# A decoder block on one core: the compressed branch's inner products in four pieces of sixteen records, without the break in the middle of each

## The chip, the cores and the metric

The kernel runs on one core of one Trainium2 chip. The metric is the device time of one execution in microseconds (us); the median of three runs is compared. Engines are called as in the profile: PE (TensorE matmul), PEld (its weight load), DVE (VectorE), ACT (ScalarE), POOL (GpSimd), SP (SyncE, which issues the loads here).

## What is computed

One block of a decoder, with 256 tokens of 1024 channels in f32. Two token mixers read one normed and modulated input h through one projection; their outputs are merged by gates and go through one output projection; a gated MLP follows. Cut to what matters:

```
mod = silu(c) @ ada_w + ada_b                      # six vectors of 1024
h   = rmsnorm(x) * (1 + scale_m) + shift_m
p   = split(h @ w_in)      # nsa_q, k/v for three branches, gates, mla parts, merge_a, merge_b
kc  = compress(p.k_cmp);  vc = compress(p.v_cmp)   # blocks of 32 tokens, stride 16: 15 per group
      # compress: gelu((block + pos) @ w1) @ w2,  w1 is 2048 x 256
o_nsa = g0 * softmax_c(q kc) vc + g1 * softmax_selected + g2 * softmax_window   # 16 heads
o_mla = mla(rmsnorm(cq) @ w_uq, rmsnorm(ckv) @ w_ukv, k_rope)                   # 8 heads
y   = sigmoid(merge_a) * o_nsa + sigmoid(merge_b) * o_mla
x   = x + gate_m * (y @ w_o)
x   = x + gate_f * convglu(rmsnorm(x) * (1 + scale_f) + shift_f)                # D_FF = 2816
out = rmsnorm(x)
```

With 256 tokens there are four selection blocks and all are taken, so the selected branch is causal attention; the window of 512 holds all tokens as well.

## The kernel before

Activations stand transposed, channels on partitions and the 256 tokens along the free axis. Most weights are loaded raw (tiles of 128x1024, 512 KB, five buffers `raw`) in one order on SP's queue, and split into a high part on ACT (`hi`, line 136) and a low part on DVE (`lo`, line 137); a product is then three on PE (`mm3`, lines 179 to 182, on top of `mm`, lines 176 and 177). The tiles of the compressed branch's `w1` are used raw.

The program's stages are: the first norm and the part of the adaLN vectors that it needs; the combined input projection; the loop over eight pairs of NSA heads; eight MLA heads, with the merge_b projections between; w_o with the residual; the feed-forward part from about 238 us on, in 22 tiles; the last norm.

The pair loop carries a second stream of work. `ORDER` (line 54) is the order of steps of one pair: turns T, logits L, values V, the finish C, and five F. At each F, `fill(1)` does the next step of `WORK` (line 53): "C0 A A A A A A A L0 C1 L1 A C2 A L2 C3 N M0 KR CK CS M1 A CR M2 Q0 CL UK A A Q1 M3 M7 M5 M6 UV M4". A step that is a generator takes a slot for each of its yields and one for its end. There are 8 x 5 = 40 slots; what is left over is done by `fill(99)` behind the loop. C0 to C3 are `cmp_mlp(c)` (from line 658): the inner layer of the compressed branch, 32 products in all, which add up in one PSUM bank `ms` (64 rows for the keys, 64 for the values, 256 columns). C3 goes on with the gelu and two transposes (line 683). L0 to L2 and M0 to M7 are projections (the MLA latents, merge_a), N the two MLA norms (lines 222, 259, 260, 271 and 273), KR the rotary key, CK the compressed keys, CS the logits and softmax of the compressed branch (lines 726 to 742), CR the turning of its rows (lines 749 and 751), Q0, Q1, UK and UV MLA's inner projections. A is one product of an adaLN tile with the condition, on DVE (a gemv, line 378), whose tile is loaded at line 534 into one of two buffers `ad`; A takes no slot.

CR sets `done`. A head pair that finishes before that is added to the list `late`: its compressed part is made by CL afterwards, two products to a pair and an add on DVE (line 768). A pair that finishes later has these two products in its own bank `o`.

What an engine does in which order is settled by a scheduler: each instruction has a priority of its kind (`PR` and `PK`, lines 50 and 51; the inner products are of the kind CM), and of what is ready the most urgent one goes first. So the slot of a step sets about where it can stand, not its exact place. In the MLA heads, line 956 is the merge (tanh gate times `o`), line 957 the add to the NSA output, lines 958 and 959 its split; line 992 is the first residual of w_o.

Of the kernel before, what the change touches and what calls it, by code (L numbers as in the profile page):

```python
# [56 lines left out]
def body(tc, a, out, dbg=None):  # L57
    nc = tc.nc
    with ExitStack() as ctx:
# [12 lines left out]
        def prio(key):  # L72
            o = PR[PK.index(key)]
            return tc.high_priority(offset=o) if o else nullcontext()
# [23 lines left out]
        def t1(tag, dt=F32, shape=(128, 256), bufs=2):  # L98
            return tp.tile(list(shape), dt, tag=tag, name=nm(tag), bufs=bufs)

        def bank(tag):
            return pa.tile([128, 512], F32, tag=tag, name=nm(tag), bufs={"lg": 2, "pt": 2, "mm": 2}.get(tag, 1))

        def free(ap, dims, off=0):
            return bass.AP(tensor=ap.tensor, offset=ap.offset + off, ap=[ap.ap[0]] + [list(d) for d in dims])
# [36 lines left out]
        def nextw():  # L142
            prefetch(depth[0])
            return pending.pop(0)
# [31 lines left out]
        def mm(o, l, r, start, stop, **kw):  # L176
            nc.tensor.matmul(o, l, r, start=start, stop=stop, **kw)  # L177
# [480 lines left out]
        def cmp_mlp(c):  # L658

            if c == 0:  # L660
                hps.append(bank("ms"))
            ps = hps[0]
            w1 = [nextw() for _ in range(2)]
            for m4 in range(4):
                m = c * 4 + m4
                for kv in range(2):
                    with prio("CM"):
                        mm(ps[kv * 64:kv * 64 + 64, 0:256], free(TB[kv][:, m // 8, :], [[8, 64]], m % 8),
                           w1[kv][:, m4 * 256:m4 * 256 + 256], m == 0, m == 15, skip_group_check=True)
                if m4 == 1:  # L670
                    yield
            if c < 3:
                return
            hx, u = t1("zh", bufs=3), t1("zh", bufs=3)
            nc.scalar.activation(hx[:], ps[:, 0:256], AF.Copy, scale=0.5)
            nc.vector.tensor_tensor(u[:], hx[:], hx[:], ALU.mult)
            nc.vector.tensor_scalar(u[:], u[:], 4 * 0.044715, 1.0, ALU.mult, ALU.add)
            nc.vector.tensor_tensor(u[:], u[:], hx[:], ALU.mult)
            nc.scalar.activation(u[:], u[:], AF.Tanh, scale=2 * float(np.float32(np.sqrt(2 / np.pi))))
            nc.vector.scalar_tensor_tensor(hx[:], u[:], 1.0, hx[:], ALU.add, ALU.mult)  # L680
            pt = bank("ms")
            for k in range(2):
                nc.tensor.transpose(pt[:, k * 128:k * 128 + 128], hx[:, k * 128:k * 128 + 128], ident)
            hT = t1("uu", F32, (128, 2, 2, 64))
            nc.scalar.activation(hT[:].rearrange("p k v c -> p (k v c)"), pt[:, 0:256], AF.Copy)
            hid.append(hT)
# [86 lines left out]
        for i in range(8):  # L773
            steps[f"M{i}"] = lambda i=i: merge_a(i)
            if i < 4:
                steps[f"C{i}"] = lambda i=i: cmp_mlp(i)
# [448 lines left out]
```

## Time and profile before

| what | us |
|---|---|
| median of three runs | 458.65 (456.47 to 459.42) |
| the profiled execution | 456.98 |
| its span | 455.2 |

The profiled execution is one run with a profile; its span is the time from the first to the last instruction, and 1.8 us lie around it. The span's mean granted clock is 0.985. A row of the profile names the line of a helper where one records all products (line 177), so that products are told apart by the names of their tiles: `mm` for projections, `lg` for logits, `pt` for transposes, `o` for values, `ms` for small things. Most products of PE appear as one record; one whose output has 64 rows appears as two.

### The profile page before, as it was taken

The numbers are of one execution on the slowest core, as the hardware profiler recorded it, in microseconds if no ns is written. First come the engines' busy times: TensorE is split into PE (matmuls) and PEld (weight loads), VectorE is DVE, ScalarE is ACT, GpSimd is POOL, SyncE is SP. The second block draws the span as 40 slices with busy tenths as digits, with TensorE's granted clock in tenths as the row PEclk, the third lists the DMA queues.
The fourth block names the chain that finished last, engine by engine and source line by source line (L and its number), as shares of the span: only waits on it lengthen the run. The fifth ranks groups of instructions, "written<-read, shape, count | busy, mean of one in ns | idle before, by whom it ended". The sixth has DMA issues, their size and how long they took to land.

```text
span 455.2 us, 8734 instructions
## 1 busy us (share of the span) xinstructions
PE 437.4 (96%) x3226; PEld 399.6 (88%) x3226; DVE 367.3 (81%) x853; ACT 288.2 (63%) x636; POOL 26.3 (6%) x45
## 2 busy tenths in 40 slices
PE   6999989999989999989999999999999999999994
PEld 6899988777869979989989999899999999999993
DVE  3799988877888887889989789987877867768643
ACT  4344475878888997556738587865656656646332
POOL 1100033030010111000000000000000000000001
PEclk8799999999999999999999999999999999999998
DMA  8999898878863337888875735885665664663002
GB/s 278 412 388 354 278 320 236 309 247 266 301 218 108 97 101 248 301 299 260 261 289 181 247 115 157 268 286 181 190 203 163 196 215 152 203 205 96 0 1 92
DMA packets 31562, 99.28 MB, mean 218 GB/s; under 512 B 4293, under 2 KB 6933, under 8 KB 31520
## 3 DMA queue, kind: packets, MB, share of 16 engines
q1 hardware_dynamic: 30208, 96.59, 63.7%
q0 software_dynamic: 1024, 1.98, 2.0%
q8 instruction: 25, 0.41, 0.4%
q10 hardware_dynamic: 288, 0.17, 0.2%
q14 instruction: 17, 0.14, 0.1%
HBM read 96.01 MB, written 1.14 MB: 213 GB/s over the span
## 4 chain that ended last, share of the span: by engine, by line
PE 78%; DVE 8%; ACT 5%; DMA 3%; issue 3%; POOL 1%; DVEq 0%; POOLq 0%; ACTq 0%
PE mm L177 30%; PE lg L177 13%; PE o L177 11%; PE ms L177 10%; PE pt L177 10%; DMA ad<-in_adaR 2%; PE pt L861 2%; DVE s L137 1%; DMA cst<-in_cst 1%; ACT hi L136 1%; DVE lo L137 1%; PE ms L222 1%; PE lg L283 1%; DVE ad L378 1%; DVE sq L1030 1%
## 5 line engine op out<-in xcount | busy, mean ns | idle before, releaser
L177 PE MATMUL mm<-s,hi 128*128 128x256 f32 x552 | 105.3, 288 | 1.0 <-ACT s L958 0.6
L177 PE MATMUL mm<-s,s 128*128 128x512 f32 (+3 forms) x400 | 92.8, 323 | 0.2 <-DVE s L1032 0.2
L137 DVE TENSOR_TENSOR s<-raw,s 128x1024 fp32r<-128x1024 f32 x66 | 80.5, 1221 | 13.0 <-PE mm L177 12.9
L177 PEld LDWEIGHTS mm<-s,hi 128*128 128x128 f32 x552 | 85.4, 189 | 4.1 <-issue 0.9
L177 PE MATMUL mm<-s,lo 128*128 128x256 f32 x268 | 76.9, 287 | 0.0
L136 ACT ACTIVATE s<-raw 128x1024 fp32r<-128x1024 f32 x66 | 69.1, 1055 | 1.9 <-PE pt L177 0.5
L137 DVE TENSOR_TENSOR lo<-raw,hi 128x1024 fp32r<-128x1024 f32 (+2 forms) x55 | 63.5, 1161 | 5.6 <-ACT hi L136 5.4
L136 ACT ACTIVATE hi<-raw 128x1024 fp32r<-128x1024 f32 (+2 forms) x55 | 53.4, 988 | 21.8 <-PE mm L177 6.8
L177 PEld LDWEIGHTS mm<-s,s 128*128 128x128 f32 x400 | 59.8, 188 | 5.8 <-DVE s L1032 0.4
L177 PEld LDWEIGHTS mm<-s,lo 128*128 128x128 f32 x268 | 50.5, 188 | 1.3 <-issue 0.7
L378 DVE CUSTOM_DVE_ANT_0 ad<-ad,crow 128x1024 f32<-128x1024 f32 x36 | 43.6, 1219 | 6.2 <-DMA ad<-in_adaR 6.2
L177 PE MATMUL o<-s,s 128*128 128x512 f32 (+2 forms) x200 | 46.9, 322 | 0.0
L177 PE MATMUL ms<-s,s 128*128 128x512 f32 (+1 forms) x192 | 45.2, 323 | 0.0
L177 PE MATMUL lg<-zh,s 128*128 128x256 f32 x176 | 34.8, 280 | 0.0
L177 PE MATMUL pt<-zh,s 128*128 128x256 f32 x176 | 34.7, 280 | 0.0
L177 PEld LDWEIGHTS o<-s,s 128*128 128x128 f32 x200 | 30.1, 188 | 3.1
L177 PEld LDWEIGHTS ms<-s,s 128*128 128x128 f32 x192 | 28.9, 188 | 3.2
L177 PEld LDWEIGHTS lg<-zh,s 128*128 128x128 f32 x176 | 28.5, 188 | 0.8
L840 ACT ACTIVATE L<-L,sm 128x128 f32<-128x128 f32 (+1 forms) x64 | 28.4, 449 | 0.5 <-DVE sm L836 0.5
L177 PEld LDWEIGHTS pt<-zh,s 128*128 128x128 f32 x176 | 28.5, 188 | 0.0
L177 PE MATMUL lg<-s,s 128*128 128x256 f32 (+4 forms) x104 | 27.3, 350 | 0.0
L177 PE MATMUL o<-pt,s 128*64 128x128 f32 (+1 forms) x224 | 24.5, 292 | 2.4 <-DVE mg L956 1.3
(260 smaller groups left out, 819.3 us busy)
## 6 DMA issues: line engine op xcount, KB each, us to landing
ad<-in_adaR SPq DMA_DIRECT2D x32, 512.0 KB, 4.9
raw<-in_wg SPq DMA_DIRECT2D x22, 512.0 KB, 3.5
raw<-in_wu SPq DMA_DIRECT2D x22, 512.0 KB, 4.4
raw<-in_wd SPq DMA_DIRECT2D x22, 512.0 KB, 4.6
raw<-in_wA SPq DMA_DIRECT2D x16, 512.0 KB, 8.0
raw<-in_wm SPq DMA_DIRECT2D x16, 512.0 KB, 5.1
L<-in_adaA SPq DMA_DIRECT2D x12, 512.0 KB, 7.8
raw<-in_cw SPq DMA_DIRECT2D x8, 512.0 KB, 5.2
```

What stands on the lines that cost most here:

```text
L136: nc.scalar.activation(hi[:], raw[:], AF.Copy)
L137: nc.vector.tensor_tensor(lo[:], raw[:], hi[:], ALU.subtract)
L177: nc.tensor.matmul(o, l, r, start=start, stop=stop, **kw)
L222: m = nc.tensor.matmul(self.ps[:, tt:tt + 1], sq[:, tt * 128:tt * 128 + 128], ones[:, 0:1], start=first and tt == 0, stop=last, skip_group ...
L283: last.append(nc.tensor.matmul(warm[:, 0:128], ones[:], ones[:], start=True, stop=True).ins)
L378: nc.vector.tensor_tensor_reduce(out=ad, in0=ad, in1=crow[:], scale=1.0, scalar=0.0, op0=ALU.mult, op1=ALU.add, accum_out=dst)
L840: nc.scalar.activation(L[:, br, j, 0:nk], L[:, br, j, 0:nk], AF.Exp, scale=-1.0, bias=sm[:, i:i + 1], accum_out=sm[:, 4 + i:5 + i])
L861: nc.tensor.transpose(pt[:, (kb * 2 + j) * 128:(kb * 2 + j) * 128 + 128], self.L[qt][:, br, j, kb * 128:kb * 128 + 128], ident)
L1030: nc.vector.scalar_tensor_tensor(v[:], x1[:, t, :], af[:, t:t + 1], rs[:], ALU.mult, ALU.mult)
```

## The change

The break in `cmp_mlp(c)` goes. Each of C0 to C3 takes one slot of the pair loop where it took two, and so all steps behind them come earlier by one to four slots.

```diff
@@ -667,8 +667,6 @@ def cmp_mlp(c)
                         mm(ps[kv * 64:kv * 64 + 64, 0:256], free(TB[kv][:, m // 8, :], [[8, 64]], m % 8),
                            w1[kv][:, m4 * 256:m4 * 256 + 256], m == 0, m == 15, skip_group_check=True)
-                if m4 == 1:
-                    yield
             if c < 3:
                 return
```

Lines behind 670 have numbers that are lower by two in the changed kernel.

Before, the list has 54 steps in slots: 40 are done in the loop, 14 behind it. After, it has 49, and 9 are left. CR stands in the 26th slot before (in pair 5) and in the 22nd after (in pair 4), so that five pairs are late before and four after.

The third piece of the inner products (C2) on PE: `ms_1111` is its bank, `raw_1230` and `raw_1289` are its weights, `lg` and `pt` belong to the attention of a head pair. Before:

```order
L177 MATMUL ms_1111<-raw_1230,s_126_790 64x256
L177 MATMUL lg_1248<-s_123_787,s_119_783 128x256
L177 MATMUL lg_1248<-s_125_789,s_119_783 128x256
L177 MATMUL ms_1111<-raw_1289,s_127_791 64x256
L177 MATMUL ms_1111<-raw_1230,s_126_790 64x256
L177 MATMUL ms_1111<-raw_1289,s_127_791 64x256
L177 MATMUL lg_1318<-s_123_787,s_119_783 128x512
L177 MATMUL lg_1318<-s_125_789,s_119_783 128x512
L177 MATMUL ms_1111<-raw_1230,s_126_790 64x256
```

The same piece after, where its weights are `raw_1226` and `raw_1241`:

```order
L177 MATMUL ms_1111<-raw_1226,s_126_790 64x256
L177 MATMUL ms_1111<-raw_1241,s_127_791 64x256
L177 MATMUL ms_1111<-raw_1226,s_126_790 64x256
L177 MATMUL ms_1111<-raw_1241,s_127_791 64x256
L177 MATMUL ms_1111<-raw_1226,s_126_790 64x256
L177 MATMUL lg_1267<-s_123_787,s_119_783 128x256
L177 MATMUL lg_1267<-s_125_789,s_119_783 128x256
L177 MATMUL ms_1111<-raw_1241,s_127_791 64x256
```

Five products now stand in a row where the logits came between after the first and after the fourth.

The stretch of the MLA norms on PE: `ms_1513` (after: `ms_1468`) is the bank of the sum of squares, `ms_1528` (after: `ms_1483`) that of the spread of the factor, `mm_1659` is the projection that stands between. Before:

```order
L222 MATMUL ms_1513<-ones,sq_1518 128x1 x2
L861 MATMUL pt_1645<-cst,L_1423 128x128
L861 MATMUL pt_1652<-cst,L_1423 128x128 x4
L177 MATMUL mm_1659<-s_16_161,hi_1458 128x256
...
L177 MATMUL mm_1659<-s_19_164,hi_1458 128x256
L273 MATMUL ms_1528<-sq_1525,ones 128x256
```

After, where the two projections are `mm_1519` and `mm_1582`:

```order
L222 MATMUL ms_1468<-ones,sq_1473 128x1 x2
L177 MATMUL mm_1519<-s_17_162,hi_1402 128x256
L177 MATMUL mm_1519<-s_19_164,hi_1402 128x256
L177 MATMUL mm_1519<-s_17_162,lo_1403 128x256
L177 MATMUL mm_1582<-s_16_161,hi_1408 128x256
...
L177 MATMUL mm_1582<-s_17_162,hi_1408 128x256
L273 MATMUL ms_1483<-sq_1480,ones 128x256
```

Between the sum and the spread stood five transposes and 12 products; now 3 and 11 products stand there, and no transpose.

The end of the last MLA head on DVE: line 378 is a gemv of adaLN, `mg` the merge, `mm_3026` (after: `mm_3024`) the first product of w_o. Before:

```order
L378 ISA ad_3876,mod<-ad_3876,crow 128x1024
L378 ISA mod 128x1
L956 SCALAR_TENSOR_TENSOR mg_2923<-mg_2923,o_2956 128x256
L378 ISA ad_3974,mod<-ad_3974,crow 128x1024
L378 ISA mod 128x1
L957 TENSOR_TENSOR s_162_1022<-s_162_1022,mg_2923 128x256
L959 TENSOR_TENSOR s_441_2490<-s_162_1022,s_439_2488 128x256
L992 SCALAR_TENSOR_TENSOR s_542_3004<-mm_3026,mod,s_542_3004 128x256
```

After:

```order
L378 ISA ad_3972,mod<-ad_3972,crow 128x1024
L378 ISA mod 128x1
L378 ISA ad_4070,mod<-ad_4070,crow 128x1024
L378 ISA mod 128x1
L954 SCALAR_TENSOR_TENSOR mg_2921<-mg_2921,o_2954 128x256
L545 TENSOR_TENSOR mod<-mod,par 128x8
L955 TENSOR_TENSOR s_162_1022<-s_162_1022,mg_2921 128x256
L1080 TENSOR_SCALAR mod<-mod 128x8
L957 TENSOR_TENSOR s_440_2488<-s_162_1022,s_438_2486 128x256
L990 SCALAR_TENSOR_TENSOR s_541_3002<-mm_3024,mod,s_541_3002 128x256
```

Two gemvs now stand ahead of the last merge and none between the merge and its add.

## Rows read from the trace of the kernel before

**Rows 1.** Busy time by stage; columns in the first row, counts in brackets.

```profile
core 0: us, PE busy (x) PEld busy (x) DVE busy (x) ACT busy (x) POOL busy (x), PEclk, DMA share, GB/s
80.00:125.00 45.00, 45.00 (x327) 34.84 (x325) 36.05 (x148) 37.18 (x116) 4.94 (x10) 1.00 0.81 280
125.00:136.00 11.00, 9.36 (x72) 7.30 (x72) 9.32 (x30) 9.72 (x33) 1.72 (x2) 1.00 0.64 211
136.00:156.00 20.00, 20.00 (x181) 18.37 (x182) 17.02 (x73) 17.89 (x60) 0.00 (x0) 1.00 0.30 99
156.00:172.00 16.00, 15.22 (x131) 11.94 (x132) 12.20 (x48) 15.26 (x46) 3.13 (x6) 1.00 0.46 126
172.00:202.00 30.00, 28.65 (x229) 27.01 (x226) 25.54 (x50) 18.80 (x39) 1.99 (x4) 1.00 0.84 286
202.00:238.00 36.00, 35.42 (x260) 32.75 (x260) 33.40 (x92) 19.57 (x58) 0.00 (x0) 1.00 0.86 277
238.00:440.00 202.00, 201.48 (x1422) 188.53 (x1422) 160.45 (x276) 125.50 (x213) 0.71 (x1) 1.00 0.55 173
```

**Rows 2.** Timeline of PE: start, us, instruction, in square brackets the idle time before.

```profile
117.44 0.40 PE L177 MATMUL mm<-s,hi 128*128 128x256 f32 x2
...
131.15 1.09 PE L177 MATMUL o<-pt,s 128*64 128x128 f32 x16 [0.81 <-ACT pt L865]
...
134.72 0.66 PE L177 MATMUL ms<-uu,w2k 128*128 128x64 f32 x4 [0.57 <-DVE s L595]
...
159.85 0.65 PE L177 MATMUL o<-Pc,s 128*64 128x256 f32 x4 [0.60 <-ACT Pc L751]
...
202.00 0.89 PE L177 MATMUL o<-pt,s 128*128 128x256 f32 x4 [1.35 <-DVE mg L956]
...
236.83 0.84 PE L177 MATMUL mm<-s,hi 128*128 128x256 f32 x3 [0.56 <-ACT s L958]
...
238.37 0.50 PE L177 MATMUL mm<-s,hi 128*128 128x256 f32 x2 [0.34 <-DVE s L992]
```

**Rows 3.** Chain of waits, 135 to 242 us: start, us, what held it.

```profile
195.29 4.87 DMA ad<-in_adaR
...
230.09 4.64 DMA ad<-in_adaR
```

**Rows 4.** Timeline of DVE.

```profile
114.60 1.22 DVE L137 TENSOR_TENSOR lo<-raw,hi 128x1024 fp32r<-128x1024 f32 x1
...
146.41 0.52 DVE L726 TENSOR_TENSOR zh<-ms,s 128x28 f32<-128x28 f32 x4 [1.57 <-PE ms L177]
...
156.58 0.40 DVE L742 TENSOR_TENSOR zh<-zh,zc 128x240 f32<-128x240 f32 x1
...
201.44 0.42 DVE L956 SCALAR_TENSOR_TENSOR mg<-mg,o 128x256 f32<-128x256 f32 x1
...
233.60 0.42 DVE L956 SCALAR_TENSOR_TENSOR mg<-mg,o 128x256 f32<-128x256 f32 x1
234.75 1.23 DVE L378 CUSTOM_DVE_ANT_0 ad<-ad,crow 128x1024 f32<-128x1024 f32 x1 [0.73 <-DMA ad<-in_adaR]
```

**Rows 5.** Instructions on the bank `ms`, 80 to 120 us: the inner products.

```profile
L177 PE MATMUL ms<-raw,s x64: 379/379/500, 80.3 to 116.8; 128*64 128x256 f32 x64
```

**Rows 6.** Chain of waits, 80 to 135 us: start, us, what, records.

```profile
81.85 0.64 PE ms L177 x4
...
84.91 0.64 PE ms L177 x2
...
91.59 1.93 PE ms L177 x14
...
121.19 1.41 PE mm L177 x12
...
126.00 0.96 POOL rv L260
```

**Rows 7.** Timeline of ACT: the split of M0's weights.

```profile
113.29 1.06 ACT L136 ACTIVATE hi<-raw 128x1024 fp32r<-128x1024 f32 x1 [1.83 <-DMA raw<-in_wm]
```

## The prediction, made before the changed kernel was timed

> **What bounds the kernel now.** I read the busy time of the engines by stage first, because the share over the whole span mixes stages. In the two stages of attention, 80 to 238 us, TensorE (PE) works 153.65 of 158 us; the other engines leave more room (DVE 133.53, ACT 118.42), and the granted clock is 1.00 everywhere [rows 1]. From 238 us on the feed-forward part is PE alone (201.48 of 202 us), and the change doesn't touch it. So a gain can come from two places only: PE work that goes away, and the 4.35 us in which PE stands idle between 80 and 238. Next I looked where those are. The table has 0 in 80 to 125 and in 136 to 156, 1.64 in 125 to 136, 0.78 in 156 to 172, 1.35 in 172 to 202 and 0.58 in 202 to 238 [rows 1]. The timeline of PE names them: 0.81 and 0.57 in the stretch of the MLA norms, 0.60 ahead of the first products on the compressed rows, 1.35 ahead of the first MLA head's second value product, 0.56 and 0.34 where the last MLA head hands over to w_o [rows 2]. The chain of waits then says what is behind the last three: the load of a tile of the adaLN matrix, 4.87 and 4.64 us long, whose product on DVE (a gemv) stands ahead of the merge that PE wants [rows 3]. A gemv holds DVE for 1.23 us; the merges of the first and the last head start at 201.44 and 233.60 [rows 4], 32.2 us for seven heads or 4.6 us a head, about the time of one such load. That tail is the most delicate place of the program.
>
> **The change part by part.** Durations are those of the profiled execution, 456.98 us (a span of 455.2 and 1.8 around it); the median of three runs, 458.65, is 1.67 longer. I sum against 456.98 and add 1.67.
>
> *A, the pieces themselves.* The removed break makes a piece of C0 to C3 eight products in one slot and not four. No product goes: all 32 (64 records, two to a product) remain [rows 5]. But they are cheaper side by side. On the chain, a run of one product costs 0.64 us, of two 0.64 as well, of seven 1.93 [rows 6]: 0.21 us for the run and 0.43 for every two products or part of two. Before there are 14 runs (3, 2, 3, 1, 7, 1, 3, 3, 1, 3, 1, 1, 2, 1: 22 pairs), after 11 (3, 2, 3, 1, 7, 5, 1, 1, 1, 1, 7: 21 pairs). C0 and C1 hardly change, since the scheduler's priorities had already packed them; C2 and C3 do. 3 x 0.21 + 0.43 = 1.06 us less of PE time, in a stretch where PE is never idle, so it counts in full. I take -1.0, between -1.1 and 0 (nothing, if the cost of a run belongs to its neighbours).
>
> Here a rule speaks for less. The Trainium skill, TensorEngine Tiling (Array Packing), section Tiling Modes, says that a change of the tiling mode drains TensorE, while another tile of one mode does not. The changes between half-width and full-width products fall from 67 to 65 only, since half-width value products often stand beside these pieces. At half of the run's 0.21 for each change that would be 0.21 and the 0.43, 0.64 instead of 1.06; the sum would be -0.5 instead of -0.9. The rows above are of runs, not of modes, and can't tell the two apart.
>
> *B, the slots.* Four slots go, and with them every later step of the list moves up. The list has 54 steps for 40 slots before (14 are left after the loop) and 49 after (9 left), because CR now falls into pair 4 and not 5: one pair less is late. Its add on DVE, as long as a merge's (0.42 us, [rows 4]), goes, and two products write to another bank. PE's work is the same; DVE was not the limit there, so B is 0 by itself. What it moves is priced in C to F. About 28 products of 128x256 move from behind the loop into it, at 0.12 us each (1.41 us for 12, [rows 6]) 3.3 us, which PE does earlier instead of later: nothing in sum.
>
> *C, the MLA norms (125 to 136 us before).* Their chain runs PE, ACT, POOL (0.96 us, [rows 6]), ACT, PE, and PE fills the time with other products. In the first turn it had five transposes and 12 products of 0.12, some 2.0 us; now 14 products, 1.65: 0.3 us more idle. The second turn loses three value products and two transposes, but its 0.81 was put down to an attention evacuation, which the new order needn't repeat: 0.1. I take +0.4. Below, the idle 1.64 could be filled wholly; above, ACT now has the split of M2's weights (1.06 us, and 1.83 of waiting for its load where a split like it waited before, [rows 7]) ahead of the second turn's step: +3.2 with the 0.4. The row nearest is the stretch as it was, so I stay near 0.
>
> *D, the compressed softmax.* Its row work on DVE, with what is mixed in, took from 146.41 to 156.98 [rows 4], 10.6 us, while PE was busy 20.00 of 20 us; only 0.60 was left behind it [rows 1, 2]. In the new order I count 7.7 to 8.5 us of PE work between the products on the keys and the second turn of the rows, and 8.9 us of DVE work to cover. 0.4 to 1.2 is missing; the products on the rows follow closely. I take +0.6, between -0.6 (the old wait goes) and +1.8 (1.2 and another 0.6).
>
> *E, weights earlier.* The first M0 product moves from 117.44 [rows 2] to about 114.3: 1.55 us of other attention work (four logit products, eight transposes) and A's share fall behind it. Its weights landed at 113.29, ACT having waited 1.83 for them [rows 7], and DVE had the low half at 115.8 [rows 4]. SP issues its load one adaLN tile earlier now, so the landing comes earlier as well. If it came no earlier, PE would stand 1.5 us. I take +0.3, between 0 and 1.5. The key rope's weights had been split long before PE took them.
>
> *F, the tail.* PE's 3.3 us less behind the loop meet a DVE that has two gemvs and one split of 1.22 fewer there (19 to 17, 16 to 15), 3.7 us; the balance stays. But between the first head's merge and the first residual of w_o there are nine gemvs where there were eight, and right ahead of the last merge stand two where there was one. The waits of 1.35, 0.56 and 0.34 make 2.25. I expect the first to go, because the gemvs ahead of it come earlier, and some 1.05 to be left at the end: -1.2, between -2.25 and +1.5 (each wait kept, and another like the 1.35).
>
> Sum: -1.0 + 0 + 0.4 + 0.6 + 0.3 - 1.2 = -0.9: 456.1 on the profiled execution's ground, 457.8 on the median's.
>
> **The rivals.** *Holes filled.* All of A, C's 1.64, D's 0.60 and F's 2.25 are gained: -5.5, 453.1 us. For it: with steps coming earlier PE has more ready products in each hole. Against it: each hole is a chain over other engines, and the new order puts less PE work beside two of them.
>
> *The tail becomes bound by the adaLN loads* (slower). A load may only start when a gemv has freed one of two buffers, and lands 4.64 to 4.87 us later [rows 3], while a head has 4.6. With nine gemvs in the place of eight and fewer products of w_o left to run ahead (12 instead of 28), each merge that stands behind a gemv not yet fed stops PE, as the one at 202.00 did for 1.35 us. Four such stops are 5.4; with A, C, D and E (+0.3) that is +5.7, 464.4 us. It decides from the point where the load lands later than DVE reaches its gemv for several heads running. Against it: before, only one of the eight gemvs there waited, for 0.73 us [rows 4].
>
> *The change does little but renumber.* PE is full, the pieces were bunched by priorities already, A's gain lies in the neighbours: 0, 458.65 us.
>
> **How the numbers follow.** The forecast has 0.42, holes filled 0.18, the tail 0.24, no effect 0.16. A measurement of this kernel can tell about 1% from no change, 454.1 to 463.2 us: the forecast and no effect (0.58) lie within it, holes filled (0.18) is faster, the tail (0.24) slower. The range goes from 453.0, just beyond the filled holes, to 464.8, just beyond the tail's price; about 0.09 lies below and 0.1 above. The forecast's own range, with each term near its middle, is 455.5 to 460.
>
> **What would show it.** In the changed kernel's profile, A is right if PE's time in the 32 products and around them shrinks by about 1 us and no idle time stands between 80 and M0's first product; E is wrong if PE waits for DVE's low half there. C and D show as PE idle time in the stretches of the norms (about 2 us) and of the rows (about 1.2). F is right if the first merge no longer stops PE and the last heads cost about 1 us; the tail rival if several merges are put down to adaLN loads. The forecast is wrong if PE's idle time between 80 us and the first w_o product is under 2 or over 8 us, or if PE's busy time in the span moves by more than 2 us.

## The result and the profile after

The changed kernel takes 461.62 us in the median (459.42 at the least, 18 runs), the kernel before 457.0 in as many; the ratio is 1.0103 with a 95% interval of 1.0081 to 1.0124. It is slower by 4.6 us, clear of no change by that interval; the forecast said 0.9 faster. The profile shown here is of an execution of 461.55 us (span 459.8). The one that came with the result ran 469.02, with 20.5 us at half of PE's clock between 80 and 245 us where this one has 3.4, and is not read for sums.

Busy time by stage of the changed kernel, with columns as in [rows 1]. The MLA norms end at about 129 us here:

```profile
80.00:125.00 45.00, 44.88 (x331) 36.20 (x332) 35.30 (x133) 37.03 (x113) 5.92 (x12) 1.00 0.79 285
125.00:129.00 4.00, 2.70 (x16) 1.62 (x17) 2.23 (x11) 2.93 (x9) 0.99 (x1) 1.00 0.86 288
129.00:133.00 4.00, 4.00 (x23) 3.34 (x23) 3.35 (x13) 3.33 (x14) 0.00 (x0) 0.57 0.27 108
133.00:136.00 3.00, 3.00 (x26) 2.91 (x26) 2.63 (x17) 3.00 (x12) 0.00 (x0) 1.00 0.00 0
136.00:156.00 20.00, 19.04 (x166) 16.73 (x164) 15.55 (x63) 15.13 (x48) 0.00 (x0) 1.00 0.39 132
156.00:172.00 16.00, 14.06 (x129) 11.33 (x130) 13.45 (x57) 14.96 (x46) 3.13 (x6) 1.00 0.41 125
172.00:202.00 30.00, 29.82 (x229) 26.33 (x228) 24.84 (x56) 20.93 (x52) 2.09 (x4) 1.00 0.77 254
202.00:242.00 40.00, 37.07 (x279) 34.63 (x277) 36.41 (x98) 20.94 (x60) 0.00 (x0) 1.00 0.80 274
```

One row has no counterpart before: from 129 to 133 us the granted clock is 0.57, that is, the clock stands at 1.2 GHz for some 3.4 us of that stretch and at 2.4 GHz for the rest (called half clock from here on). PE is busy throughout, so the busy share hides it. Ahead of it stand 1.3 us of waiting in 125 to 129.

PE's waits on its timeline, to be held against [rows 2]:

```profile
126.77 0.70 PE L273 MATMUL ms<-sq,ones 128*128 128x256 f32 x2 [0.73 <-ACT sq L271]
128.04 0.43 PE L177 MATMUL ms<-uu,w2k 128*128 128x64 f32 x2 [0.57 <-DVE s L595]
...
145.13 1.96 PE L177 MATMUL ms<-KB,s 128*128 128x32 f32 x16 [0.50 <-DVE s L706]
...
156.73 0.41 PE L747 MATMUL ms<-cst,zh 128*128 128x128 f32 x2 [1.03 <-DVE zh L740]
...
158.12 0.65 PE L177 MATMUL o<-Pc,s 128*64 128x256 f32 x4 [0.52 <-ACT Pc L749]
...
170.36 1.09 PE L177 MATMUL o<-pt,s 128*64 128x128 f32 x16 [0.51 <-ACT pt L863]
...
211.46 0.33 PE L937 MATMUL pt<-cst,L 128*128 128x128 f32 x1 [1.38 <-DVE L L934]
...
241.58 0.85 PE L177 MATMUL mm<-s,hi 128*128 128x256 f32 x3 [1.46 <-ACT s L956]
```

The norms wait as before (1.30; 1.38 before). New are 0.50 ahead of the compressed logits, 1.03 at the second turn of the rows, 0.51 in the attention behind; the wait ahead of the first merge is gone, but 1.38 stand at 211.46 and the last grew from 0.56 to 1.46.

What is behind the last is seen on DVE, where two gemvs stand in a row ahead of the merge (L954) and the second waits for its load:

```profile
236.67 1.22 DVE L378 CUSTOM_DVE_ANT_0 ad<-ad,crow 128x1024 f32<-128x1024 f32 x1
...
239.05 1.23 DVE L378 CUSTOM_DVE_ANT_0 ad<-ad,crow 128x1024 f32<-128x1024 f32 x1 [1.15 <-DMA ad<-in_adaR]
...
240.20 0.42 DVE L954 SCALAR_TENSOR_TENSOR mg<-mg,o 128x256 f32<-128x256 f32 x1
```

The sum is read best from the first inner product to the start of the first w_o product behind the last merge. The first row is the kernel before; the other two are executions of the changed one, of 459.94 us (one of the runs below) and of 461.55:

```profile
80.28:236.82 156.54, 152.20 (x1185) 131.38 (x1184) 132.67 (x437) 118.03 (x345) 11.78 (x22) 1.00 0.72 237
```

```profile
79.80:239.95 160.15, 152.70 (x1185) 131.75 (x1184) 133.12 (x440) 118.08 (x345) 12.12 (x22) 1.00 0.69 233
```

```profile
79.92:241.57 161.65, 154.23 (x1185) 132.87 (x1184) 133.43 (x441) 118.26 (x345) 12.12 (x22) 0.99 0.68 233
```

The same PE instructions; PE waits 4.34 us before and 7.45 and 7.42 after: 3.1 more. PE's own time, that is the stretch without its waits, is 0.5 longer in the execution without half clock there, and another 1.53 in the one with it. That is the 3.6 or 5.1 us of the stretch. From there to the end all three take 218.2 to 218.4 us.

### The profile page after: what moved, and what is told of

It is laid out like the page before. It is cut to its first block, busy times and chain, and to the rows that moved or that the text cites. A ratio compares the mean times of both kernels' runs of the same rounds, so it can differ in the third digit from the quotient of the medians.

```text
span 467.2 us, 8722 instructions
## 1 busy us (share of the span) xinstructions
PE 445.5 (95%) x3226; PEld 407.6 (87%) x3226; DVE 366.7 (78%) x852; ACT 288.6 (62%) x636; POOL 26.6 (6%) x45
## 4 chain that ended last, share of the span: by engine, by line
PE 73%; DVE 10%; ACT 5%; issue 5%; DMA 4%; POOL 1%; DVEq 0%; POOLq 0%; ACTq 0%
PE mm L177 27%; PE lg L177 12%; PE o L177 10%; PE ms L177 10%; PE pt L177 10%; DMA ad<-in_adaR 3%; PE pt L859 2%; DVE lo L137 2%; ACT hi L136 1%; DVE s L137 1%; DMA cst<-in_cst 1%; ACT L L838 1%; PE ms L222 1%; DVE sq L1028 1%; DVE ad L378 1%
## 5 line engine op out<-in xcount | busy, mean ns | idle before, releaser
L177 PE MATMUL mm<-s,hi 128*128 128x256 f32 x552 | 109.8, 296 | 1.7 <-ACT s L956 1.1
L177 PEld LDWEIGHTS mm<-s,hi 128*128 128x128 f32 x552 | 88.3, 195 | 5.6 <-issue 1.7
L177 PE MATMUL mm<-s,lo 128*128 128x256 f32 x268 | 78.6, 294 | 0.0
L177 PEld LDWEIGHTS mm<-s,lo 128*128 128x128 f32 x268 | 52.1, 194 | 1.4 <-issue 0.9
L834 DVE CUSTOM_DVE_ANT_0 L<-lg,s 128x128 f32<-128x128 f32 (+1 forms) x64 | 20.7, 350 | 8.8 <-PE lg L177 8.8
L177 PE MATMUL o<-pt,s 128*64 128x128 f32 (+1 forms) x224 | 26.3, 308 | 0.7 <-ACT pt L863 0.5
```

What stands on the lines that cost most here:

```text
L834: nc.vector.tensor_tensor_reduce(out=L[:, br, j, 0:nk], in0=lgj[:, br, :], in1=bias_view(2 * t + j, qt), scale=1.0, scalar=3e38, op0=ALU.a ...
```

## The experiments

In the lists of steps E is an empty slot (a step that does nothing). Edits are against the changed kernel unless it is said otherwise.

**The changed kernel again**, twice; no edit.

> The changed kernel once more, for a second profile. All theories: about 1% over the kernel before. Tail theory (the adaLN loads hold up DVE, and DVE holds up the MLA heads): of PE's idle time between 80 us and the first residual of w_o, 3.5 us or more lie in the MLA heads, 2.25 before. Middle theory (the compressed softmax and the norms lost their cover): more than half of the idle time that is new lies ahead of the MLA heads. Pieces theory (eight products in one slot are worse by themselves): PE's own time from 80 us to the norms is longer by a microsecond or more, without a wait.

> The changed kernel on the same chip as the other three, as their measure: ratio 1.008 to 1.012. Theory of the norms' hole: half clock for 3.4 us between 127 and 133 us in this profile too.

The first is a single run of 461.55 us, the profile above; the second gave 1.0092 (1.0058 to 1.0127). The waits in the MLA heads are 3.19 us, short of the tail theory's 3.5, and of the 3.1 us of new waits 2.1 lie ahead of them, as the middle theory had it. No single place has all of them. The half clock, there in the first profile, is missing in the second (459.94 us), whose row of 129 to 133 has 1.00:

```profile
129.00:133.00 4.00, 4.00 (x34) 3.58 (x34) 3.94 (x19) 4.00 (x17) 0.00 (x0) 1.00 0.20 81
```

Two executions of one program (on two chips), with the same waits within 0.1 us, differ by 1.6 us; 34 records instead of 23 in the four microseconds show where. The half clock that the second expectation has in its last sentence did not come.

**Whole pieces in the old slots.**

```diff
-WORK = "C0 A A A A A A A L0 C1 L1 A C2 A L2 C3 N M0 KR CK CS M1 A CR M2 Q0 CL UK A A Q1 M3 M7 M5 M6 UV M4"
+WORK = "C0 E A A A A A A A L0 C1 E L1 A C2 E A L2 C3 E N M0 KR CK CS M1 A CR M2 Q0 CL UK A A Q1 M3 M7 M5 M6 UV M4"
```

> Pieces whole, but an empty slot behind each of C0 to C3, so that all later steps stand in the slots they had before. Pieces theory: the loss stays, about +4.6 us (ratio 1.010). Tail and middle theory: the loss goes, and the 1 us of joined runs may show: ratio 0.997 to 1.001.

1.0016 (0.9987 to 1.0044): the loss goes. So it is the slots that cost, not the eight products together. The microsecond of the joined runs doesn't show in the time. From start to start the 32 products take 10.87 us instead of 11.61, 0.7 less, but M0's products now come too early for their weights:

```profile
110.86 0.39 PE L177 MATMUL mm<-s,lo 128*128 128x256 f32 x1 [1.62 <-DVE lo L137]
```

**One, two and three slots earlier.**

```diff
+one:   "C0 E A A A A A A A L0 C1 E L1 A C2 E A L2 C3 N M0 ..."
+two:   "C0 E A A A A A A A L0 C1 E L1 A C2 A L2 C3 N M0 ..."
+three: "C0 E A A A A A A A L0 C1 L1 A C2 A L2 C3 N M0 ..."
```

> Pieces whole, an empty slot behind C0, C1 and C2, none behind C3: everything from the norms on is one slot earlier than before. By the written order some 6.7 us of PE work stand between the products on the compressed keys and the second turn of the rows (6.5 before, 3.8 changed). Cover theory (the loss is that PE has too little else to do while DVE makes the compressed softmax and while the norms go through ACT and POOL): near before, ratio 0.998 to 1.003. Tail theory (gemvs of adaLN ahead of the MLA merges): eight gemvs in the tail as before, 0.998 to 1.003 as well. Slot theory (each slot by which the steps come earlier costs its share): 1.002 to 1.004.

> Two slots earlier from the third piece on. 4.5 us of PE work at the compressed softmax, seven gemvs in the tail. Cover theory: ratio 1.004 to 1.009, with 1 us or more of idle PE at the second turn of the rows or behind it. Tail theory: 0.997 to 1.002. Slot theory: 1.004 to 1.006.

> Three slots earlier from the second piece on. 4.5 us of PE work at the compressed softmax, eight gemvs in the tail. Cover theory: 1.004 to 1.009, idle PE at the rows as in the run with two. Tail theory: 0.998 to 1.003. Slot theory: 1.007 to 1.009.

1.0042 (1.0019 to 1.0066), 1.0026 (1.0002 to 1.0051) and 1.0051 (1.0019 to 1.0082), against 1.0103 for four. No theory has all three in its range: a price for each slot asks for 1.004 or more with two (1.0026), and the cover and tail theories ask for 1.003 or less with one (1.0042). But the intervals are too wide to exclude any of them, and they overlap, so that the order among the three is not settled either. At the softmax (145 to 158 us) PE waits 1.0, 2.0 and 1.5 us in their profiles, against 2.2. Each list is dealt anew by the scheduler, and each has other waits.

Nor are waits all that a list sets. Over the same 1230 products, from the first inner product on, one slot and three slots have these rows:

```profile
81.19:243.94 162.75, 156.98 (x1232) 135.94 (x1231) 139.06 (x451) 122.49 (x353) 11.44 (x22) 1.00 0.70 235
```

```profile
79.72:244.06 164.34, 160.75 (x1231) 138.39 (x1231) 138.66 (x451) 122.47 (x352) 11.57 (x22) 1.00 0.69 229
```

Three slots wait less (3.6 us for 5.8), yet PE's own time is 3.8 us longer, both at full clock. By the same count it is 158.5 before and 158.7 in the changed kernel without half clock. So the order in which the products stand has a price of its own, of the size of that of the waits. What makes it was not tested.

**The tail in the old slots, the rest as changed.**

```diff
-... M1 A CR M2 Q0 CL UK A A Q1 ...
+... M1 A CR E E E E M2 Q0 CL E UK A A Q1 ...
```

> The changed kernel with four empty slots behind CR and one behind CL, so that everything up to CR stands as in the changed kernel and everything behind it in the slots of before. Tail theory: most of the loss goes, ratio 0.998 to 1.004, and PE's idle time in the MLA heads is back near 2.3 us. Middle theory: the loss stays, ratio 1.007 to 1.011. Pieces theory: the loss stays, 1.010.

1.0096 (1.0064 to 1.0129): the loss stays, though PE waits nowhere in the MLA heads. This spoke against the tail theory, but the empty slots deal the second half of the pair loop anew as well, where its profile (of 457.96 us, the least of ten runs, so no measure of the sum) has these waits:

```profile
153.41 0.75 PE L859 MATMUL pt<-cst,L 128*128 128x128 f32 x4 [0.78 <-ACT L L850]
...
156.64 0.51 PE L177 MATMUL mm<-s,hi 128*128 128x256 f32 x2 [0.93 <-DVE gg L561]
```

So it shows that a tail without waits is not enough, and no more.

**Two more gemvs in the loop.** This touches the tail alone: up to 157 us the changed kernel's waits stand unchanged.

```diff
-... CL UK A A Q1 ...
+... CL UK A A A A Q1 ...
```

> The changed kernel with two more gemvs of adaLN in the loop's list, behind UK: norms and softmax stand as in the changed kernel, and ahead of the last merge is one gemv where there are three. Cover theory: the loss stays but for a microsecond, ratio 1.007 to 1.010. Tail theory: 1.002 to 1.006, and the waits of 1.38 and 1.46 us in the MLA heads go. Slot theory: 1.010.

> Two more gemvs in the loop once more, as the measure of the other two on one chip: ratio 1.003 to 1.007, waits at the compressed rows as in the changed kernel (1.03 and 0.5 us), waits in the tail under 1 us.

1.0052 (1.0012 to 1.0092) and 1.0031 (1.0006 to 1.0057): half or more of the loss comes back, as the tail theory had it. In the second profile the one wait of the whole tail is

```profile
237.24 0.50 PE L177 MATMUL mm<-s,hi 128*128 128x256 f32 x2 [0.34 <-DVE s L990]
```

against 1.38, 1.46 and 0.35 in the changed kernel, 2.85 less; in time 2.3 to 3.3 us. The waits are not the whole of it: over the same 1230 products PE's own time is 1.2 us shorter as well (157.5 in the first profile for 158.7 in the changed kernel, both without half clock). The 4.5 us of waits up to the tail are as many as in the changed kernel. What is left of the loss is in part the half clock, which this profile has behind the compressed keys:

```profile
142.00:150.00 8.00, 8.00 (x65) 7.64 (x65) 4.56 (x20) 3.60 (x12) 0.00 (x0) 0.79 0.40 100
```

**The same edit on the kernel before.**

> The kernel before with two more gemvs of adaLN in the loop. Tail theory: the wait of 1.35 us ahead of the first merge and the one at the end go or shrink, ratio 0.996 to 0.999. If these waits are only moved to another place: 0.999 to 1.003.

1.0021 (0.9994 to 1.0048): nothing is gained. The 1.35 and 0.56 are gone, but the MLA heads now wait elsewhere:

```profile
201.53 0.34 PE L939 MATMUL pt<-cst,L 128*128 128x128 f32 x1 [0.40 <-DVE L L936]
205.62 0.33 PE L939 MATMUL pt<-cst,L 128*128 128x128 f32 x1 [0.35 <-DVE L L936]
...
226.12 0.70 PE L177 MATMUL lg<-s,s 96*128 96x256 f32 x2 [0.37 <-DVE sm L925]
```

**One slot ahead of CR.**

```diff
-... CS M1 A CR M2 ...
+... CS M1 A E CR M2 ...
```

> The changed kernel with one empty slot ahead of CR. No gemv is moved in the list, but by the order one gemv stands ahead of the last MLA merge where the changed kernel has three, and eight between the first merge and w_o. Tail theory: ratio 1.003 to 1.007 as with the moved gemvs, the waits of 1.4 and 1.5 us in the tail gone. If it was not the tail's gemvs but something else that the two moved gemvs changed: 1.008 to 1.011.

1.0075 (1.0051 to 1.0099), between the two expectations. The tail's waits are gone without a gemv moved in the list, but for 0.19 at the last merge and w_o's own 0.35. At the rows the wait grew from 1.03 to 1.61, and the 0.50 ahead of the keys is gone:

```profile
156.15 0.50 PE L177 MATMUL mm<-s,hi 128*128 128x256 f32 x2 [1.61 <-DVE gg L561]
...
239.02 0.39 PE L177 MATMUL mm<-s,hi 128*128 128x256 f32 x1 [0.19 <-ACT s L956]
```

On the same chip the second run with two gemvs was 2.3 us faster in the median, and waits don't explain it. The same 1230 products, there and here:

```profile
78.18:242.08 163.90, 159.09 (x1232) 138.58 (x1232) 138.36 (x449) 123.02 (x353) 12.02 (x22) 0.99 0.69 231
```

```profile
79.61:246.01 166.40, 161.41 (x1231) 138.77 (x1231) 139.65 (x451) 122.50 (x353) 12.02 (x22) 0.99 0.69 229
```

The waits are 4.8 and 5.0 us, the half clock is 3.4 us in both, and PE's own time differs by 2.3.

**No gemv in the softmax.**

```diff
-... CS M1 A CR M2 Q0 CL UK A A Q1 ...
+... CS M1 CR M2 Q0 CL UK A A A A A Q1 ...
```

> Three more gemvs behind UK, one of them taken from between M1 and CR, so that none stands on DVE in the compressed softmax. Softmax theory (PE waits at the rows because DVE has 1.2 us too much there): the waits at the rows, 1.5 us, fall under 0.7, ratio 0.8 to 1.5 us under the run with two gemvs, 0.999 to 1.004. If PE has less to do there instead (2.9 us where 3.8 stood by the order): the waits stay, ratio as the run with two gemvs.

1.0083 (1.0058 to 1.0109), a miss on both sides. With DVE relieved of 1.2 us the wait at the rows is longer (by the order PE has less other work there, 2.9 us where 3.8 stood), and a wait in the tail is back:

```profile
156.91 0.73 PE L177 MATMUL lg<-s,s 128*128 128x512 f32 x2 [1.95 <-DVE sm L834]
...
214.71 0.33 PE L937 MATMUL pt<-cst,L 128*128 128x128 f32 x1 [1.46 <-DVE L L934]
```

So one gemv is not what holds up the softmax. What its waits are worth in time was not separated by any run.

**M0 ahead of the norms**, alone and with the two gemvs.

```diff
-... C3 N M0 KR ...
+... C3 M0 N KR ...
```

> The changed kernel with M0 ahead of N in the list. Ahead of the second spread of the norms PE has 1.75 us of other products where the changed kernel has 1.24 and the kernel before 1.66; softmax and tail stand as in the changed kernel. Theory of the norms' hole (PE's waits of 0.73 and 0.57 us there, and the 3.4 us at half clock that begin within 1.5 us behind them in three of four profiles with this order): the waits shrink, no half clock at 125 to 135 us, ratio 1.003 to 1.007. Tail theory: 1.008 to 1.011. Softmax theory (the waits at the compressed rows make the rest): 1.008 to 1.011.

> M0 ahead of N, and two more gemvs of adaLN in the loop. If norms and tail are both causes and add up: ratio 0.998 to 1.003, with the waits at the compressed rows (2 us in all) as what is left. If only the tail counts: 1.004 to 1.006. If only the norms: 1.003 to 1.007.

1.0196 (1.0158 to 1.0234) and 1.0081 (1.0048 to 1.0113). The norms' waits are gone as expected (10.95 of 11 us busy), and so is the half clock there; but now PE waits for the compressed keys, and the half clock begins behind that:

```profile
125.00:136.00 11.00, 10.95 (x82) 9.30 (x82) 8.30 (x32) 9.74 (x32) 0.75 (x1) 1.00 0.39 140
136.00:146.00 10.00, 9.01 (x78) 7.58 (x76) 8.23 (x35) 8.87 (x29) 0.00 (x0) 1.00 0.51 157
146.00:154.00 8.00, 8.00 (x52) 7.63 (x51) 4.07 (x18) 4.47 (x15) 0.00 (x0) 0.57 0.31 92
```

The time was expected lower and is higher. The half clock is 6.8 us here, and over the same 1230 products PE's own time, with half of that taken off as an estimate for full clock, is 160.9 us, 2.2 more than in the changed kernel. The two gemvs are worth 5 us here, more than the 2.5 of tail waits (0.90 and 1.61) that go with them. Between the two profiles the same 1230 products differ by 5.7 us: 2.8 of waits, 1.7 by 3.4 us less of half clock, 1.2 of PE's own time.

**A longer norm chain in the kernel before.** DVE keeps its order row for row, and so does PE but for the two products of the second spread, which stand three products later. A factor times 1.0 is added twice on POOL in each of the two MLA norms.

```diff
             nc.gpsimd.tensor_tensor(v[:, 2:4], v[:, 0:2], mhalf[:], ALU.pow)
+            for i in range(extra):   # 2 in the MLA norms
+                nc.gpsimd.tensor_scalar(v[:, 2:4], v[:, 2:4], 1.0, None, ALU.mult)
```

> The kernel before, in the same order on PE and DVE, with two more small steps on POOL in each of the two MLA norms (a factor times 1.0), so that PE waits longer in the stretch of the norms: 0.3 to 1.5 us more idle time a turn by the length of such a step, which no row shows yet (the power step beside it takes 0.70 to 1.44). Theory that longer waits of PE there bring the half clock: a stretch of 3.4 us at half clock behind 125 us in the profile, which none of the profiles of the old order has, and a time longer than the added waits by about 1.7 us: ratio 1.004 to 1.010. Rival, that waits alone don't do it: no half clock there, and the time is longer by the added waits only: ratio 1.001 to 1.006.

1.0079 (1.0049 to 1.0109), 4.0 us in the medians. On POOL the two steps take 1.24 us:

```profile
127.81 1.24 POOL L262 TENSOR_SCALAR rv<-rv 128x2 f32<-128x2 f32 x2
133.61 1.17 POOL L260 TENSOR_TENSOR rv<-rv,mhalf 128x2 f32<-128x2 f32 x1 [4.56 <-ACT rv L259]
134.87 1.24 POOL L262 TENSOR_SCALAR rv<-rv 128x2 f32<-128x2 f32 x2
```

PE's waits there:

```profile
129.82 0.70 PE L275 MATMUL ms<-sq,ones 128*128 128x256 f32 x2 [1.07 <-ACT sq L273]
...
136.89 0.70 PE L275 MATMUL ms<-sq,ones 128*128 128x256 f32 x2 [1.77 <-ACT sq L273]
138.16 1.07 PE L177 MATMUL ms<-uu,w2k 128*128 128x64 f32 x4 [0.58 <-DVE s L597]
```

and right behind them the clock:

```profile
138.00:145.00 7.00, 6.84 (x32) 5.73 (x33) 5.24 (x24) 6.88 (x25) 0.00 (x0) 0.52 0.14 50
```

In an order that had not shown it in any profile, longer waits are followed by 6.8 us of half clock. PE idles 3.90 of 13 us in 125 to 138, against 1.64 before: 2.3 us of waits explain only a part of the 4.0. A second stretch of half clock, 3.4 us, comes behind waits of 0.93 and 0.34 us where w_o begins:

```profile
244.00:248.00 4.00, 4.00 (x23) 4.00 (x22) 4.00 (x8) 2.38 (x6) 0.00 (x0) 0.57 0.15 15
```

The ratio alone would fit the rival too (up to 1.006); the clock rows speak for the theory. They are of one execution, of 463.47 us, 2.9 above the median of its runs, and how often the others met the half clock is not known.

All profiles together: with the changed order up to the norms (or M0 ahead of them) eight of ten have a stretch at half clock between 125 and 163 us, behind waits at the norms (four), the keys (three) or the rows (one). Of the old order and one to three slots less, six profiles in all, none has, and the longer chain has. What makes two of the ten go without is open: one is the second profile of the changed kernel, with the same waits. Waits alone don't settle it: the list with one slot less waits 1.8 us in the norms without it, and the list with two has the changed kernel's pair of waits there (0.75 and 0.57) without it.

## Why the prediction was wrong

*A* has the right number, in part by luck. Predicted was -1.0. From start to start the 64 records of the 32 products take 11.61 us before and 10.43 in the execution without half clock, -1.2. The chain of the changed kernel:

```profile
91.29 1.94 PE ms L177 x14
93.65 1.50 PE ms L177 x10
...
110.62 1.47 PE ms L177 x13
```

Runs of seven and five products cost 1.94 and 1.50, as 0.21 and 0.43 a pair give. But joining them was not what gained: C2, with its run of five and three single products, takes 3.42 us for 3.12 before, and the whole gain is C3's, 1.65 for 3.13. The price of runs gives 2.57 for C3. The last row is most of C3, between half-width value products: 0.23 for each product and nothing for the entry. Here the trace agrees with the rule that was weighed, of the Trainium skill, TensorEngine Tiling (Array Packing), section Tiling Modes: the entry is paid where the width changes. The changes counted by it are 65, yet the gain was no smaller than by runs.

*B* was wrong in one sentence: "PE's work is the same". The 573 projection products of 128x256 take 75.4 us from start to start, waits left out, before and 77.5 in the changed kernel (no half clock). They stand in 72 runs instead of 63, and the longest run behind the loop, where one costs 0.12, has 60 of them instead of 102; the others moved in among attention products. With A's gain and small differences of other products, PE's time is 0.5 longer where A promised 1.0 less.

*C* had the waits about right, +0.4 against -0.2 (1.42 idle, small gaps included, for 1.64), but had no term for the clock. That the waits of PE have a second price, 1.5 us of half clock behind them, was nowhere in the sum; no row before showed it at that place. The chain also grew on POOL: the second power step takes 1.44 us, 0.77 before, beside a low-half split on DVE. The row before, then the two of the changed kernel:

```profile
131.90 0.77 POOL L260 TENSOR_TENSOR rv<-rv,mhalf 128x2 f32<-128x2 f32 x1 [4.95 <-ACT rv L259]
```

```profile
124.55 1.44 POOL L260 TENSOR_TENSOR rv<-rv,mhalf 128x2 f32<-128x2 f32 x1 [3.78 <-ACT rv L259]
```

```profile
124.22 1.22 DVE L137 TENSOR_TENSOR lo<-raw,hi 128x1024 fp32r<-128x1024 f32 x1
```

(C's upper bound has a slip: 1.06, 1.83 and 0.4 make 3.3 and not 3.2, which changes nothing.)

*D* was under-sized: +0.6, measured 0.50 + 0.17 + 1.03 + 0.52 = 2.2 for 0.60, +1.6, inside its bounds (to +1.8). The count of what was missing, 0.4 to 1.2, was right for the wait on the turn (1.03); that the rows' evacuation (0.52) stays beside it, and that the keys wait too, was not counted. *E* was nearly right: PE doesn't wait for M0's weights (44.88 of 45 us busy), 0 for +0.3. In the attention behind the rows 0.7 us of waits are new, for which the sum had no term.

*F* failed, with the sign: -1.2 predicted, +0.9 measured. The step that failed is "I expect the first to go ... and some 1.05 to be left at the end". The first went. But another of its size came at the second head (1.38: on DVE a gemv, the merge and two splits stand ahead, without a pause from 207.00 us on), and the one at the last merge didn't shrink but grew from 0.56 to 1.46, as the two gemvs in a row, seen in the order, should have told. The 0.34 that F counted with them is w_o's own: it stands at 0.34 or 0.35 in the changed kernel and with two gemvs moved alike. Moving two gemvs brought back 2.3 to 3.3 us, which shows that the tail's waits count; a part of it is PE's own time.

So the terms are -1.2, +1.7, -0.2, +1.6, 0, +0.7, +0.9 and +1.5 for the clock: 5.0 of the 5.1 us in that stretch, where the forecast had -0.9. Of the difference F is 2.1, B 1.7, the clock 1.5, D 1.0 and the attention behind the rows 0.7; C, E and A give 1.1 back. The rival of the tail named a mechanism that is seen, but with 5.4 us of stops it was over-sized: two stops, not four, and a gemv that waits long for its load (1.15 us) only at the second of them. No single rival came. The time lies inside the range (453.0 to 464.8) by a sum of small losses that the forecast had near zero, and not because the sum was right. The forecast's own signs of being wrong were set too wide to catch it: the idle time of 7.4 us is under its limit of 8, and PE's busy time in the stretch moved by 0.5 us, or by 2.0 with the half clock, for a limit of 2.

## What to carry to other kernels

Where an engine is 97% busy and a list of slots feeds a scheduler, removing slots gains what the instructions themselves get cheaper, and pays with whatever the new deal uncovers: here pieces that were 1.2 us cheaper came with a loss of 4.6. Look in the new order for what stands ahead of the waited-for instruction on an in-order engine: two gemvs ahead of a merge, the second behind its load, were visible before any run. Don't take the engine's own time as given either: here the same 1230 products took PE 157.0 to 160.8 us at full clock, by their order. And a wait of TensorE can cost more than its length: eight of ten profiles of the changed order have a stretch at half clock behind such waits.

## What was not expected of the hardware

Waits of PE of 1.3 us in 125 to 129 were followed by 3.4 us at half clock in one execution (0.57 in 129 to 133) and by none in another, and the longer waits of the last run by 6.8 us (0.52 in 138 to 145). In the first pair the difference was 1.5 us of PE time and 1.6 us in all. The Trainium skill, TensorE: Matmul & The Clock Gate, section HAM oscillation, says that waits inside a kernel can bring the clock back down and that the price is then paid again; it tells of DMA waits in every turn of a loop. The traces agree in kind, with two waits of 0.73 and 0.57 us, and show besides that one program may or may not meet it.

In the MLA norms the power step on POOL took 0.69 to 0.78 us in half of the rows and 1.43 or 1.44 in the eight profiles in which a split with two operands in SBUF had begun on DVE some 0.3 us before it. The others lie between; one is 0.95, in the first norm of the kernel before, where a split ran on DVE as well. The Trainium skill, SBUF — State Buffer, section SBUF: two separate sides, says that such a DVE instruction and GpSimd lock each other out for a whole instruction. The rows agree in kind: the power step of 1.44 us ends 0.55 us behind the split. No run here separated the two.
